# Last stage of a hybrid decoder step: the tokens divided 384/160 in the place of 272/272

## The chip, the core and the metric

The kernel runs on one core of a Trainium2 chip. The core has five engines that run side by side, each with its own stream of instructions: TensorE (PE, the matmuls, with PEld for its weight loads), VectorE (DVE), ScalarE (ACT), GpSimd (POOL) and SyncE (SP, which in this kernel issues most of the DMAs). Data lies in SBUF, matmul results in PSUM, inputs and outputs in the memory outside. The metric is the device time of one execution in microseconds (us), and less is better.

## What is computed

One layer of a decoder trunk for 512 prompt tokens and 32 sample tokens (8 sequences of 4), 544 tokens in all, with a model width of 2048 and a hidden width of 8192. What matters here is the end, the product with `w_down` and the final norm:

```
h = rms_norm(x, norm_ffn_w)
x = x + square(relu(h @ w_up)) @ w_down
y = rms_norm(x, final_norm_w)      # x * rsqrt(mean(x*x) + EPS) * w, for each token over 2048 values
```

Values are float32. The kernel gets that from products of rounded parts: a weight tile and an activation tile are each split into a high part (rounded) and a low part (the rest), and a product is three matmuls, high x high, high x low and low x high.

## The kernel before

Features lie on the 128 partitions, tokens on the free dimension. The 544 tokens are two halves of HT = 272 columns (256 prompt and 16 sample tokens each). The 2048 output features are KT = 16 blocks of 128; two blocks share a tile, `x2p[pair]`, with the layout pair member, half, token. The largest part of the product with `w_down` runs ahead of the last stage with fewer, combined products. The last stage adds what is left: four blocks of 128 hidden features (two stored activation tiles, STORED), which give `u`, four pairs of a high and a low part.

The last stage is the loop over `steps` (L1338 and on): for each half h, for each pair q of output blocks, for each of the two blocks ob:

- 12 matmuls (`product`, four hidden blocks times three parts) of 272 columns each into one bank of PSUM (`ps_small`, `ps_sm` in the trace), each matmul with its own weight load of 128 columns;
- `add` (L919): DVE adds the bank to `x2[ob][:, h]`, after which the bank is free;
- ACT squares the sum (`sq`, L1349) and multiplies it by the norm's weight (L1350);
- POOL adds the squares up in `ssq` (L1354), except those of the last two blocks, which stay separate.

The pool `small` has four banks, given out in turn, to the norms too. So output k can start when the addition of output k - 4 is done, one step earlier behind a norm.

`rstd_rows` is the norm of a half: three full-precision matmuls with a matrix of ones sum the squares over the partitions (each matmul is two records in the trace), ACT does Ln and Exp (L179, L180), DVE one refining step in four instructions (L181 to L184). Then `finish` (L1317 and on) multiplies a pair of blocks by the result, 2 x 272 columns on DVE (L1319), and SP stores it (L1320): eight multiplies and eight stores for each half. The norm of half 0 is written behind the second output of half 1, and its multiplies and stores between the later outputs. The norm of half 1, its eight multiplies and its eight stores come behind the last product.

The weights (`last_weight`, tile `w_raw`, split by ACT L992 and DVE L993) are loaded and split during half 0 and kept for half 1. A scheduler sets the order in which each engine gets its instructions, from its own estimates; `urgent()` gives what it holds a higher priority. An engine takes its instructions in that order.

Of the kernel before, what the change touches and what calls it, by code (L numbers as in the profile page):

```python
# [13 lines left out]
AF = mybir.ActivationFunctionType  # L14
ALU = mybir.AluOpType
MUL, ADD, SUB, MIN, MAX = ALU.mult, ALU.add, ALU.subtract, ALU.min, ALU.max
PSUM, DRAM = bass.MemoryType.PSUM, bass.MemoryType.DRAM

P = 128
D = 2048  # L20
KT = D // P
# [3 lines left out]
HT = HP + HS  # L25
# [3 lines left out]
EPS = 1e-6  # L29
# [12 lines left out]
STORED = [2, NF - 1]  # L42
SPAN, RING = 6, 8
RAMP = [0, 0, 2, 2, 4, 4, 6, 6]
W_OUT_ORDER = [0, 1, 2, 3, 4, 5, 8, 9, 10, 11, 12, 13, 6, 7, 14, 15]


def ahead(items, load, depth=2):

    items, queue = list(items), []  # L50
    for i, it in enumerate(items):
        while len(queue) < min(depth + 1, len(items) - i):
            queue.append(load(items[i + len(queue)]))
        yield it, queue.pop(0)
# [3 lines left out]
def trunk(ctx, tc, a):  # L58
    nc = tc.nc
# [35 lines left out]
    def tile_in(p, name, shape, dt=F32, tag=None, bufs=None):  # L95
        return p.tile(shape, dt, tag=tag or name, name=name, bufs=bufs)
# [3 lines left out]
    def ln_exp(force=False):  # L100
        if force or table[0] != "ln_exp":
            tc.keep_in_program_order(S.preload_act_table_set("natural_log_exp_and_others"))
            table[0] = "ln_exp"
# [27 lines left out]
    def ps_small(n=512):  # L131
        return tile_in(small, "ps_sm", [P, 512], tag="sm")[:, :n]
# [38 lines left out]
    def rstd_rows(out, ssqs, t, halves=(0, 1)):  # L171

        for h in halves:
            pr = ps_small(HT)
            for i, q in enumerate(ssqs):
                PE.matmul(pr, ones, q[:, h, :], start=i == 0, stop=i == len(ssqs) - 1)
            y, th = out[:, h, :], t[:, h, :]
            ln_exp()
            S.activation(y, pr, AF.Ln, bias=eps_t, scale=1.0 / D)  # L179
            S.activation(y, y, AF.Exp, scale=-0.5)  # L180
            V.tensor_tensor(th, y, y, MUL)  # L181
            V.scalar_tensor_tensor(th, pr, EPS * D, th, ADD, MUL)
            V.tensor_scalar(th, th, -0.5 / D, 1.5, MUL, ADD)
            V.tensor_tensor(y, y, th, MUL)  # L184

    def rsqrt_cols(y, x, t):

# [1113 lines left out]
             lambda key: [combos(key[1][1] + k) for k in range(key[1][2])], down_out)  # L1301


    u = []
    for m in STORED:
        x = [tile_in(cmb2, "ux", [P, 2, HT], tag="c") for _ in range(2)]
        for i in range(2):
            nc.sync.dma_start(x[i], u_d[m][:, 2 * i : 2 * i + 2])
        for i in range(2):
            hi, lo = c_tile(hlp, "ul"), c_tile(hlp, "ul")  # L1310
            parts_into(hi, lo, x[i])
            u.append(tuple((t[:, 1], t[:, 0]) for t in (hi, lo)))
    r3 = r1
    ssq = tile_in(cmb2, "ssq3", [P, 2, HT], tag="c")
    sqs = [[ssq], [ssq]]

    def finish(h, pair):  # L1317
        t = x2p[pair][:, :, h, :]
        V.tensor_tensor(t, t, r3[:, h : h + 1, :].broadcast_to([P, 2, HT]), MUL)  # L1319
        nc.sync.dma_start(a["o_y"][pair][:, :, h, :], t)  # L1320

    w_2 = []

    def last_weight(q):

        if len(w_2) < KT:
            with urgent():
                raw = tile_in(rawp, "w_raw", [P, 1024])
                nc.sync.dma_start(raw, a["w_d2"][q])
                for j in range(2):  # L1330
                    src = raw[:, 512 * j : 512 * j + 512]
                    hi, lo = (c_tile(hlp if len(w_2) < 12 else cmb, n).rearrange("p a b -> p (a b)")[:, :512]
                              for n in ("w2_hi", "w2_lo"))
                    parts_into(hi, lo, src)
                    w_2.append((hi, lo))
        return w_2[2 * q : 2 * q + 2]

    steps = [(h, q) for h in range(2) for q in range(KT // 2)]  # L1338
    for (h, q), ws in ahead(steps, lambda it: last_weight(it[1]), 1):
        for j in range(2):  # L1340
            ob = 2 * q + j
            x = x2[ob][:, h]
            ps = ps_small(HT)
            for k in range(4):
                product({h: ps}, ws[j], k * P, u[k], k == 0, k == 3, (h,))
            add(x, ps)
            sq = tile_in(cmb2, "sq", [P, 2, HT], tag="c")
            with urgent():
                S.activation(sq[:, h], x, AF.Square)  # L1349
                S.activation(x, x, AF.Copy, scale=nv[:, 32 + ob : 33 + ob])  # L1350
            if ob == 0:
                G.tensor_copy(ssq[:, h, :], sq[:, h])
            elif ob < KT - 2:
                G.tensor_tensor(ssq[:, h, :], ssq[:, h, :], sq[:, h], ADD)  # L1354
            else:
                sqs[h].append(sq)
            if h == 1 and ob == 1:
                rstd_rows(r3, sqs[0], tile_in(cmb2, "rt", [P, 2, HT], tag="c"), (0,))
            elif h == 1 and ob % 2:
                finish(0, ob // 2 - 1)  # L1360
    finish(0, KT // 2 - 1)
    with urgent():
        rstd_rows(r3, sqs[1], tile_in(cmb2, "rt", [P, 2, HT], tag="c"), (1,))
    for o in range(KT // 2):
        finish(1, o)

# [130 lines left out]
```

## Time and profile before

| | us |
|---|---|
| median of 3 runs | 2433.86 (2429.49 to 2435.54) |
| the profiled execution | 2434.44 |
| its span | 2432.7 |
| TensorE busy in the span | 2385.1 (98%) |
| VectorE busy | 1809.2 (74%) |
| ScalarE busy | 1078.2 (44%) |
| GpSimd busy | 494.7 (20%) |
| last product issued | about 2417.6 after the start of the span |
| first multiply of the last norm | 2422.49 |

A profile shows one execution. "Busy" counts a matmul from its start to a modelled end, and matmuls overlap, so what a matmul costs in a row of matmuls is the distance between two starts. Where an engine was idle before an instruction, the row names in brackets what ended the wait. Times of rows are us from the start of the span.

### The profile page before, as it was taken

The numbers are of one execution on the slowest core, as the hardware profiler recorded it, in microseconds if no ns is written. First come the engines' busy times: TensorE is split into PE (matmuls) and PEld (weight loads), VectorE is DVE, ScalarE is ACT, GpSimd is POOL, SyncE is SP. The second block draws the span as 40 slices with busy tenths as digits, with TensorE's granted clock in tenths as the row PEclk, the third lists the DMA queues.
The fourth block names the chain that finished last, engine by engine and source line by source line (L and its number), as shares of the span: only waits on it lengthen the run. The fifth ranks groups of instructions, "written<-read, shape, count | busy, mean of one in ns | idle before, by whom it ended". The sixth has DMA issues, their size and how long they took to land.

```text
span 2432.7 us, 47364 instructions
## 1 busy us (share of the span) xinstructions
PE 2385.1 (98%) x19089; PEld 2358.4 (97%) x19089; DVE 1809.2 (74%) x2937; ACT 1078.2 (44%) x1598; POOL 494.7 (20%) x776
## 2 busy tenths in 40 slices
PE   9999999999999999998999999999999999999997
PEld 8999999999999999998999999999999999999997
DVE  9676676666657635888888888888578888888885
ACT  6424332432432424555555555555323333333445
POOL 5123213312412204310010111101401212121003
PEclk9999999999999999999999999999999999999999
DMA  6243333333333546565555555556945656565433
GB/s 203 93 115 117 98 112 109 118 98 96 126 94 108 179 127 206 189 214 192 193 193 201 201 199 187 182 191 214 391 133 169 229 165 227 160 218 152 139 94 111
DMA packets 144275, 397.96 MB, mean 164 GB/s; under 512 B 35348, under 2 KB 44216, under 8 KB 144056
## 3 DMA queue, kind: packets, MB, share of 16 engines
q1 hardware_dynamic: 108648, 266.12, 34.9%
q0 software_dynamic: 35408, 128.82, 14.1%
q8 instruction: 150, 2.46, 0.4%
q14 instruction: 69, 0.57, 0.1%
HBM read 317.37 MB, written 77.49 MB: 162 GB/s over the span
## 4 chain that ended last, share of the span: by engine, by line
PE 86%; DVE 5%; DMA 5%; ACT 2%; issue 1%; SPq 0%; DVEq 0%; POOLq 0%; ACTq 0%; POOL 0%
PE ps_s L76 49%; PE ps_big L76 30%; PE ps_sm L76 7%; DVE w_lo L145 2%; DMA w_raw<-in_w_o_dram 2%; DMA w_raw<-in_w_up_dram 2%; ACT w_hi L142 1%; DMA w_q<-in_w_up_dram 1%; DMA w_raw<-in_w_d_dram 1%; DVE x L1004 1%; DMA xr<-in_x_dram 0%; PE ps_sm L80 0%; DVE x_lo L160 0%; DVE w_lo L1130 0%; ACT w_hi L1129 0%
## 5 line engine op out<-in xcount | busy, mean ns | idle before, releaser
L1129 ACT ACTIVATE w_hi<-w_q 128x768 fp32r<-128x768 f32 (+3 forms) x422 | 375.1, 889 | 559.0 <-PE ps_s L76 466.1
L76 PE MATMUL ps_s<-uc,w_hi 128*128 128x272 f32 x3136 | 593.1, 289 | 6.9 <-ACT w_hi L1129 6.3
L76 PEld LDWEIGHTS ps_s<-uc,w_hi 128*128 128x128 f32 x3136 | 491.1, 188 | 10.6 <-ACT w_hi L1129 8.9
L1130 DVE TENSOR_TENSOR w_lo<-w_q,w_hi 128x768 fp32r<-128x768 f32 (+3 forms) x422 | 425.3, 1008 | 65.0 <-ACT w_hi L1129 63.5
L76 PE MATMUL ps_s<-uc,w_lo 128*128 128x272 f32 x1568 | 450.2, 288 | 0.0
L76 PE MATMUL ps_big<-x_hi,w_hi 128*128 128x272 f32 x2016 | 425.9, 292 | 0.6 <-ACT x_hi L157 0.5
L76 PE MATMUL ps_big<-x_hi,w_lo 128*128 128x272 f32 x2016 | 418.3, 289 | 2.6 <-DVE w_lo L145 2.6
L76 PE MATMUL ps_big<-x_lo,w_hi 128*128 128x272 f32 x2016 | 419.0, 289 | 0.3 <-DVE x_lo L160 0.3
L142 ACT ACTIVATE w_hi<-w_raw 128x1024 fp32r<-128x1024 f32 (+3 forms) x215 | 211.4, 983 | 432.4 <-PE ps_big L76 287.0
L145 DVE TENSOR_TENSOR w_lo<-w_raw,w_hi 128x1024 fp32r<-128x1024 f32 (+3 forms) x215 | 277.6, 1291 | 148.1 <-ACT w_hi L142 143.6
L76 PEld LDWEIGHTS ps_big<-x_hi,w_hi 128*128 128x128 f32 x2016 | 316.6, 188 | 5.1 <-ACT x_hi L157 1.7
L76 PEld LDWEIGHTS ps_big<-x_hi,w_lo 128*128 128x128 f32 x2016 | 315.5, 188 | 3.5 <-DVE w_lo L145 3.4
L76 PEld LDWEIGHTS ps_big<-x_lo,w_hi 128*128 128x128 f32 x2016 | 317.0, 189 | 0.7 <-DVE x_lo L160 0.5
L76 PEld LDWEIGHTS ps_s<-uc,w_lo 128*128 128x128 f32 x1568 | 294.9, 188 | 0.3 <-DVE w_lo L1130 0.3
L76 PE MATMUL ps_s<-c_hi,w_hi 128*128 128x272 f32 x928 | 267.3, 288 | 5.9 <-ACT w_hi L1129 5.7
L76 PE MATMUL ps_s<-c_hi,w_lo 128*128 128x272 f32 x928 | 268.2, 289 | 1.4 <-DVE w_lo L145 0.7
L76 PE MATMUL ps_s<-c_lo,w_hi 128*128 128x272 f32 x928 | 267.1, 288 | 0.0
L919 DVE TENSOR_TENSOR x2v<-x2v,ps_s 128x272 f32<-128x272 f32 x326 | 140.1, 434 | 74.1 <-PE ps_s L76 72.3
L1229 POOL DMA_DIRECT2D uc<-ucd x196 | 106.2, 547 | 432.7 <-PE ps_s L76 414.7
L76 PEld LDWEIGHTS ps_s<-c_hi,w_hi 128*128 128x128 f32 x928 | 175.5, 189 | 6.4 <-ACT w_hi L1129 5.9
L76 PEld LDWEIGHTS ps_s<-c_hi,w_lo 128*128 128x128 f32 x928 | 175.1, 189 | 2.1 <-DVE w_lo L1130 1.2
L76 PEld LDWEIGHTS ps_s<-c_lo,w_hi 128*128 128x128 f32 x928 | 175.1, 189 | 0.0
(375 smaller groups left out, 4223.2 us busy)
## 6 DMA issues: line engine op xcount, KB each, us to landing
w_q<-in_w_up_dram SPq DMA_DIRECT2D x116, 512.0 KB, 5.0
w_raw<-in_w_in_dram SPq DMA_DIRECT2D x106, 512.0 KB, 3.4
uc<-ucd POOLq DMA_DIRECT2D x196, 272.0 KB, 5.9
w_q<-in_w_d_dram SPq DMA_DIRECT2D x128, 384.0 KB, 3.3
w_raw<-in_w_o_dram SPq DMA_DIRECT2D x32, 512.0 KB, 3.7
ucd<-u_hi POOLq DMA_DIRECT2D x28, 544.0 KB, 5.7
ucd<-tc POOLq DMA_DIRECT2D x28, 544.0 KB, 6.8
w_raw<-in_w_up_dram SPq DMA_DIRECT2D x28, 512.0 KB, 3.6
```

The costliest lines, as they stand in the source:

```text
L76: return cls.held(nc.tensor.matmul(*args, **kw))
L142: S.activation(hi[:, c], raw[:, c], AF.Copy)
L145: V.tensor_tensor(lo[:, c], raw[:, c], hi[:, c].bitcast(F32), SUB)
L919: V.tensor_tensor(out, out, ps, ADD)
L1004: V.scalar_tensor_tensor(x2[o][:, h], x2[o][:, h], nv[:, KT + o : KT + o + 1], r2[:, h], MUL, MUL)
L1129: S.activation(hi, s, AF.Copy)
L1130: V.tensor_tensor(lo, s, hi.bitcast(F32), SUB)
L1229: nc.gpsimd.dma_start(t.bitcast(F32), uc_d[KS[j]][:, 2 * b : 2 * b + 2])
```

## The change

The last stage no longer divides the tokens at 272. Its first part has the columns 0 to 383 of the 544, its second part the 160 that remain. To take a slice of any width, the pair of halves is read as one row of 544 columns (`flat`). Products, additions, squares, sums, norms, multiplies and stores of the stage go by these parts: the same number of instructions, with 384 columns where the first half had 272 and 160 where the second half had 272. `rstd_rows` is cut in two, with the body for one slice in `rstd`. The stored activations were kept with the halves exchanged. They are now put in order as they are loaded, so that four loads of 2 x 272 columns become eight of 272.

```
+CUT = 384
...
+    def rstd(y, ssqs, th, n):
+        pr = ps_small(n)
+        for i, q in enumerate(ssqs):
+            PE.matmul(pr, ones, q, start=i == 0, stop=i == len(ssqs) - 1)
+        ln_exp()
...
         for i in range(2):
-            nc.sync.dma_start(x[i], u_d[m][:, 2 * i : 2 * i + 2])
+            for h in range(2):
+                nc.sync.dma_start(x[i][:, h], u_d[m][:, 2 * i + 1 - h])
         for i in range(2):
             hi, lo = c_tile(hlp, "ul"), c_tile(hlp, "ul")
             parts_into(hi, lo, x[i])
-            u.append(tuple((t[:, 1], t[:, 0]) for t in (hi, lo)))
-    r3 = r1
-    ssq = tile_in(cmb2, "ssq3", [P, 2, HT], tag="c")
+            u.append((flat(hi), flat(lo)))
+    r3 = flat(r1)
+    ssq = flat(tile_in(cmb2, "ssq3", [P, 2, HT], tag="c"))
     sqs = [[ssq], [ssq]]
-
-    def finish(h, pair):
-        t = x2p[pair][:, :, h, :]
-        V.tensor_tensor(t, t, r3[:, h : h + 1, :].broadcast_to([P, 2, HT]), MUL)
-        nc.sync.dma_start(a["o_y"][pair][:, :, h, :], t)
+    PARTS = (slice(0, CUT), slice(CUT, 2 * HT))
+
+    def finish(v, pair):
+        c = PARTS[v]
+        t = x2p[pair].rearrange("p j h t -> p j (h t)")[:, :, c]
+        V.tensor_tensor(t, t, r3[:, c].unsqueeze(1).broadcast_to([P, 2, c.stop - c.start]), MUL)
+        nc.sync.dma_start(a["o_y"][pair].rearrange("p j h t -> p j (h t)")[:, :, c], t)
...
-            ps = ps_small(HT)
-            for k in range(4):
-                product({h: ps}, ws[j], k * P, u[k], k == 0, k == 3, (h,))
+            ps = ps_small(c.stop - c.start)
+            whi, wlo = ws[j]
+            for k, (xhi, xlo) in enumerate(u):
+                for i, (wp, xp) in enumerate(((whi, xhi), (whi, xlo), (wlo, xhi))):
+                    PE.matmul(ps, wp[:, k * P : (k + 1) * P], xp[:, c], start=k == i == 0, stop=k == 3 and i == 2)
             add(x, ps)
...
-            if h == 1 and ob == 1:
-                rstd_rows(r3, sqs[0], tile_in(cmb2, "rt", [P, 2, HT], tag="c"), (0,))
-            elif h == 1 and ob % 2:
+            if v == 1 and ob == 1:
+                last_norm(0)
+            elif v == 1 and ob % 2:
                 finish(0, ob // 2 - 1)
     finish(0, KT // 2 - 1)
     with urgent():
-        rstd_rows(r3, sqs[1], tile_in(cmb2, "rt", [P, 2, HT], tag="c"), (1,))
+        last_norm(1)
```

The scheduler gives some instructions another order. On DVE, behind the norm of the first part, this stood before (L919 is the addition of an output of the second part, with `ps_sm` as its bank; L1319 is the final multiply of a pair of the first part):

```order
L182 SCALAR_TENSOR_TENSOR rt_28317<-ps_sm_28318,rt_28317 128x272
L919 TENSOR_TENSOR x2v1_19950<-x2v1_19950,ps_sm_28328 128x272
L183 TENSOR_SCALAR rt_28317<-rt_28317 128x272
L184 TENSOR_TENSOR r1_91<-r1_91,rt_28317 128x272
L1319 TENSOR_TENSOR x2v0_19948<-x2v0_19948,r1_91 128x2x272
L919 TENSOR_TENSOR x2v1_19950<-x2v1_19950,ps_sm_28346 128x272
L1319 TENSOR_TENSOR x2v1_19950<-x2v1_19950,r1_91 128x2x272
L919 TENSOR_TENSOR x2v2_19952<-x2v2_19952,ps_sm_28366 128x272
L1319 TENSOR_TENSOR x2v2_19952<-x2v2_19952,r1_91 128x2x272
L1319 TENSOR_TENSOR x2v3_19954<-x2v3_19954,r1_91 128x2x272
L919 TENSOR_TENSOR x2v2_19952<-x2v2_19952,ps_sm_28384 128x272
```

Additions and multiplies alternate: after the norm, one or two multiplies stand between two additions. At the same place on DVE there is now this (L922 the addition, L1326 the multiply):

```order
L187 TENSOR_TENSOR r1_91<-r1_91,rt_28321 128x384
L1326 TENSOR_TENSOR x2v0_19948<-x2v0_19948,r1_91 128x2x384
L922 TENSOR_TENSOR x2v1_19950<-x2v1_19950,ps_sm_28332 128x160
L1326 TENSOR_TENSOR x2v1_19950<-x2v1_19950,r1_91 128x2x384
L1326 TENSOR_TENSOR x2v2_19952<-x2v2_19952,r1_91 128x2x384
L1326 TENSOR_TENSOR x2v3_19954<-x2v3_19954,r1_91 128x2x384
L922 TENSOR_TENSOR x2v1_19950<-x2v1_19950,ps_sm_28350 128x160
L1326 TENSOR_TENSOR x2v4_20171<-x2v4_20171,r1_91 128x2x384
L1326 TENSOR_TENSOR x2v5_20173<-x2v5_20173,r1_91 128x2x384
L1326 TENSOR_TENSOR x2v6_20175<-x2v6_20175,r1_91 128x2x384
L1326 TENSOR_TENSOR x2v7_20177<-x2v7_20177,r1_91 128x2x384
L922 TENSOR_TENSOR x2v2_19952<-x2v2_19952,ps_sm_28370 128x160
```

The eight multiplies have only two additions among them, and the addition that stood among the norm's refining steps now stands behind the first multiply.

On TensorE, in the products of the very last output, the sums of squares of the second norm (`ones`) stood so before (`ul` with `w2` is a product, `ssq3` the sum of POOL, `sq` the square of output 14):

```order
L76 MATMUL ps_sm_28573<-ul_27894,w2_hi_28207 128x272
L76 MATMUL ps_sm_28595<-ssq3_27914,ones_87 128x272
L76 MATMUL ps_sm_28573<-ul_27895,w2_hi_28207 128x272
L76 MATMUL ps_sm_28573<-ul_27894,w2_lo_28208 128x272
L76 MATMUL ps_sm_28573<-ul_27898,w2_hi_28207 128x272
L76 MATMUL ps_sm_28573<-ul_27899,w2_hi_28207 128x272
L76 MATMUL ps_sm_28595<-sq_28570,ones_87 128x272
```

Four products lie between the two sums. There they stand so now:

```order
L77 MATMUL ps_sm_28577<-ul_27896,w2_hi_28211 128x160
L77 MATMUL ps_sm_28599<-ssq3_27918,ones_87 128x160
L77 MATMUL ps_sm_28577<-ul_27897,w2_hi_28211 128x160
L77 MATMUL ps_sm_28599<-sq_28574,ones_87 128x160
L77 MATMUL ps_sm_28577<-ul_27896,w2_lo_28212 128x160
```

One product lies between them. The rest of the products follows as before.

## Rows read from the trace of the kernel before

**Rows 1.** The page: the span of the profiled execution.
```profile
span 2432.7 us, 47364 instructions
```

**Rows 2.** Stages: stretch, us, busy us (instructions) of each engine, clock, DMA, GB/s.
```profile
2364.50:2390.60 26.10, 26.10 (x209) 26.10 (x209) 19.23 (x37) 20.51 (x46) 11.26 (x14) 1.00 0.42 141
2390.60:2417.90 27.30, 26.91 (x205) 26.07 (x203) 15.37 (x29) 16.09 (x35) 11.22 (x14) 1.00 0.24 83
...
2422.50:2432.70 10.20, 0.00 (x0) 0.00 (x0) 5.16 (x8) 0.00 (x0) 0.00 (x0) 0.50 0.63 219
```

**Rows 3.** Timeline of TensorE at four places: start us, us, what, count.
```profile
62.88 1.28 PE L76 MATMUL ps_sm<-sel,abr 64*128 64x16 f32 x10
...
62.88 0.50 PE L76 MATMUL ps_sm<-sel,abr 64*128 64x16 f32 x3
...
109.25 0.28 PE L76 MATMUL ps_sm<-kq_hi 128*128 128x256 f32 x1
...
109.96 0.41 PE L76 MATMUL ps_big<-x_hi,w_hi 128*128 128x272 f32 x2
...
236.31 0.39 PE L76 MATMUL ps_sm<-nl,ones_r 128*128 128x512 f32 x1
...
236.77 0.39 PE L76 MATMUL ps_sm<-nl,ones_r 128*128 128x512 f32 x1
...
2371.04 0.29 PE L76 MATMUL ps_sm<-ul,w_lo 128*128 128x272 f32 x1
...
2374.05 0.29 PE L76 MATMUL ps_sm<-ul,w_lo 128*128 128x272 f32 x1
```

**Rows 4.** Weight loads by shape: count, busy us, mean ns of one, idle before.
```profile
L76 PEld LDWEIGHTS ps_sm<-ul,w_hi 128*128 128x128 f32 x256 | 40.3, 188 | 0.2
...
L76 PEld LDWEIGHTS ps_sm<-s,km 128*64 128x64 f32 x128 | 13.8, 137 | 1.2
```

**Rows 5.** Timeline of TensorE at the two norms.
```profile
2393.75 0.62 PE L76 MATMUL ps_sm<-ssq,ones 128*128 128x272 f32 x2
...
2395.37 0.29 PE L76 MATMUL ps_sm<-ul,w_lo 128*128 128x272 f32 x1
...
2415.29 0.73 PE L76 MATMUL ps_sm<-ssq,ones 128*128 128x272 f32 x2 [0.35 <-POOL ssq L1354]
```

**Rows 6.** Timeline of DVE and POOL at the final multiplies.
```profile
2398.39 1.30 DVE L1319 TENSOR_TENSOR x2v<-x2v,r 128x544 f32<-128x544 f32 x1
...
2398.33 0.77 POOL L1354 TENSOR_TENSOR ssq<-ssq,sq 128x272 f32<-128x272 f32 x1 [2.50 <-ACT sq L1349]
...
2422.49 5.17 DVE L1319 TENSOR_TENSOR x2v<-x2v,r 128x544 f32<-128x544 f32 x8
```

**Rows 7.** The chain that ended last, behind the last product: start us, us, what.
```profile
2417.89 0.45 DVE x2v L919
...
2418.43 0.44 ACT sq L1349
...
2418.91 0.74 PE ps_sm L76 x2
...
2419.67 0.50 ACT r L179
...
2422.49 0.73 DVE x2v L1319
```

**Rows 8.** Instructions on `ul`: ns min/median/max, first and last start, form.
```profile
L992 ACT ACTIVATE ul<-ux x4: 641/642/644, 2301.9 to 2309.0; 128x544 fp32r<-128x544 f32 x4
L993 DVE TENSOR_TENSOR ul<-ux,ul x4: 718/718/718, 2302.9 to 2311.9; 128x544 fp32r<-128x544 f32 x4
```

**Rows 9.** SP's last stores, and stretches in which their data starts and ends (DMA share).
```profile
2423.28 5.33 SPq L1320 DMA_DIRECT2D out_o_y_dram<-x2v  x8
...
2424.00:2425.00 1.00, 0.00 (x0) 0.00 (x0) 1.00 (x2) 0.00 (x0) 0.00 (x0) 0.50 0.52 181
...
2430.00:2431.00 1.00, 0.00 (x0) 0.00 (x0) 0.00 (x0) 0.00 (x0) 0.00 (x0) 0.50 0.71 235
```

More of the change, by code (lines that the diff above doesn't have):

```diff
@@ L173, in rstd_rows @@
         for h in halves:
[L174 to L184, printed above, removed]
+            rstd(out[:, h, :], [q[:, h, :] for q in ssqs], t[:, h, :], HT)
+    def rstd(y, ssqs, th, n):
[3 more added lines that the diff above has]
+        ln_exp()
+        S.activation(y, pr, AF.Ln, bias=eps_t, scale=1.0 / D)
+        S.activation(y, y, AF.Exp, scale=-0.5)
+        V.tensor_tensor(th, y, y, MUL)
+        V.scalar_tensor_tensor(th, pr, EPS * D, th, ADD, MUL)
+        V.tensor_scalar(th, th, -0.5 / D, 1.5, MUL, ADD)
+        V.tensor_tensor(y, y, th, MUL)
     def rsqrt_cols(y, x, t):
@@ L1301, in trunk @@
              lambda key: [combos(key[1][1] + k) for k in range(key[1][2])], down_out)
+    flat = lambda t: t.rearrange("p h t -> p (h t)")
     u = []
@@ L1311, in trunk, with last_norm @@
             parts_into(hi, lo, x[i])
-            u.append(tuple((t[:, 1], t[:, 0]) for t in (hi, lo)))
-    r3 = r1
-    ssq = tile_in(cmb2, "ssq3", [P, 2, HT], tag="c")
+            u.append((flat(hi), flat(lo)))
+    r3 = flat(r1)
+    ssq = flat(tile_in(cmb2, "ssq3", [P, 2, HT], tag="c"))
     sqs = [[ssq], [ssq]]
-    def finish(h, pair):
-        t = x2p[pair][:, :, h, :]
-        V.tensor_tensor(t, t, r3[:, h : h + 1, :].broadcast_to([P, 2, HT]), MUL)
-        nc.sync.dma_start(a["o_y"][pair][:, :, h, :], t)
+    PARTS = (slice(0, CUT), slice(CUT, 2 * HT))
[4 more added lines that the diff above has]
+        nc.sync.dma_start(a["o_y"][pair].rearrange("p j h t -> p j (h t)")[:, :, c], t)
+    def last_norm(v):
+        c = PARTS[v]
+        t = flat(tile_in(cmb2, "rt", [P, 2, HT], tag="c"))[:, c]
+        rstd(r3[:, c], [q[:, c] for q in sqs[v]], t, c.stop - c.start)
     w_2 = []
@@ L1336, in last_weight @@
         return w_2[2 * q : 2 * q + 2]
-    steps = [(h, q) for h in range(2) for q in range(KT // 2)]
-    for (h, q), ws in ahead(steps, lambda it: last_weight(it[1]), 1):
+    steps = [(v, q) for v in range(2) for q in range(KT // 2)]
+    for (v, q), ws in ahead(steps, lambda it: last_weight(it[1]), 1):
+        c = PARTS[v]
         for j in range(2):
             ob = 2 * q + j
-            x = x2[ob][:, h]
-            ps = ps_small(HT)
-            for k in range(4):
-                product({h: ps}, ws[j], k * P, u[k], k == 0, k == 3, (h,))
+            x = flat(x2[ob])[:, c]
+            ps = ps_small(c.stop - c.start)
[3 more added lines that the diff above has]
+                    PE.matmul(ps, wp[:, k * P : (k + 1) * P], xp[:, c], start=k == i == 0, stop=k == 3 and i == 2)
             add(x, ps)
-            sq = tile_in(cmb2, "sq", [P, 2, HT], tag="c")
+            sq = flat(tile_in(cmb2, "sq", [P, 2, HT], tag="c"))
             with urgent():
-                S.activation(sq[:, h], x, AF.Square)
+                S.activation(sq[:, c], x, AF.Square)
                 S.activation(x, x, AF.Copy, scale=nv[:, 32 + ob : 33 + ob])
             if ob == 0:
-                G.tensor_copy(ssq[:, h, :], sq[:, h])
+                G.tensor_copy(ssq[:, c], sq[:, c])
             elif ob < KT - 2:
-                G.tensor_tensor(ssq[:, h, :], ssq[:, h, :], sq[:, h], ADD)
+                G.tensor_tensor(ssq[:, c], ssq[:, c], sq[:, c], ADD)
             else:
-                sqs[h].append(sq)
-            if h == 1 and ob == 1:
-                rstd_rows(r3, sqs[0], tile_in(cmb2, "rt", [P, 2, HT], tag="c"), (0,))
-            elif h == 1 and ob % 2:
+                sqs[v].append(sq)
+            if v == 1 and ob == 1:
+                last_norm(0)
+            elif v == 1 and ob % 2:
                 finish(0, ob // 2 - 1)
```

## The prediction

> **What bounds the kernel now.** I read the span first [rows 1], then the last stage in three stretches [rows 2]: products of half 0 (in the first 26.1 us), of half 1 (27.3 us, TensorE busy 26.91), and the end, 10.2 us in which TensorE does nothing and DVE is busy for half. TensorE is granted its full 2.4 GHz in the first two (1.00). So up to 2417.9 the price of a product counts, and behind it a chain of single instructions and a queue of stores. Product prices stand in the TensorE timeline [rows 3]: a matmul starts where the one before it lets go, so the distance of two starts is the price, not the duration shown. 24 products of 272 columns lie between 2371.04 and 2374.05: 125.4 ns each. Six of 256 columns take 0.71 us, 118 ns each. Two of 512 columns take 0.46 us, 229 ns each. Between these a column costs about 0.43 ns. The small ones are another matter: ten matmuls with 16 columns take 1.28 us, the first three of them 0.50, so seven steps take 0.78 us, 112 ns each, with next to nothing to stream. What they share with the products is a weight tile of 128 columns. Its load lasts 188 ns, one of 64 columns 137 ns [rows 4]: 0.8 ns a column, about 102 ns for 128, and a fixed part that overlaps. So I read 112 ns as the floor of a step whose weights are 128 columns wide. It has never shown in this kernel's products because 256 columns or more are longer.
>
> **The change, part by part.** All times are of the profiled execution (2434.44 us, span 2432.7), which lies 0.6 us above the median of the runs, 2433.86.
>
> *Products of the first part.* 192 matmuls go from 272 to 384 columns. On the line from 125.4 to 229 ns, 384 lies at 125.4 + 112/240 x 103.6 = 173.7 ns. 192 x 48.3 ns = **+9.3 us**. From below, at 0.4167 ns a column (one column a cycle at the granted 2.4 GHz), it is +9.0. All of it is on the path, since TensorE is the bound here. ACT and DVE split weights beside it, with more time for each output than before.
>
> *Products of the second part.* 192 matmuls go from 272 to 160 columns. If they follow their columns the line gives 118 - 96 x 0.434 = 76 ns; with the floor it is 112 ns; from above, no cheaper than now, 125.4, unless narrow matmuls run in more passes (a rival below). I take 112, since those steps have the same weight width, and the products load new weights for each matmul: 192 x 13.4 ns = **-2.6 us**, with -9.5 and 0 as ends. This is the core of the forecast: the columns taken out of part 2 hardly come back as time, those put into part 1 are paid in full.
>
> The Trainium skill has a rule that speaks against this: "TensorE: Matmul & The Clock Gate", section "Back-to-back issue gap", puts an isolated gap at N/2.4 + 2.5 ns, in which the weight load has no share. An estimate by it: 384 + 160 cost the same as 272 + 272 (162.5 + 69.2 against 2 x 115.8 ns), and this and the last paragraph together come to zero. The rows say 125.4 where that rule has 115.8.
>
> *Norms.* A norm has three full-precision matmuls, six records. In the middle of half 1 they and two products take from 2393.75 to 2395.37, 1.62 us, so 0.457 us for each of the three [rows 5], in proportion to columns. Norm 0 grows by 3 x 0.19, the two of norm 1 that lie in the product stream shrink by 2 x 0.19: **+0.2 us**. Their order shifts too: the square of output 14 is now wanted behind one product instead of four. TensorE waited 0.35 us for POOL's sum there [rows 5]; it will now wait some 0.45 for the square. **+0.1**.
>
> *A wait in part 2.* The order of DVE shows it. After the first norm, the eight final multiplies of part 1 stand almost in one piece: one, the addition of output 2, three, the addition of output 3, four, the addition of output 4. Every addition frees one of four PSUM banks, and output k needs the bank of output k - 4. A multiply of 544 elements takes 0.65 us when nothing is beside it (5.17 for eight, [rows 6]), one of 768 then 0.91. From the start of part 2: two outputs 2.7 us (12 x 112 ns each), norm matmuls 1.94 to 4.65, Ln and Exp (0.59 and 0.53 with 0.09 for 112 more columns, hops) to 6.0, four DVE steps of 0.42 to 0.56 to 8.2, multiply to 9.1, addition 2 to 9.45, three multiplies and addition 3 to 12.5, four and addition 4 to 16.5. TensorE meanwhile ends output 6 at 11.4. Output 7 waits 1.1 us for the bank of output 3. It ends at 13.9, and output 8 waits 2.6 for that of output 4. Before, multiplies and additions alternate, and TensorE does not stop. In addition POOL's sums stretch multiplies that run beside them: one took 1.30 us beside a POOL addition of 0.77 [rows 6]. Two narrower ones fall into this clump, some 0.4 us each. Together **+4.5 us**; the ends are 2 (additions a little earlier than I place them) and 6.
>
> *The chain behind the last product.* 112 columns are worth 0.12 us on DVE and 0.09 on ACT: 272 elements take 0.45 and 0.44, 544 take 0.72 and 0.64 [rows 7, 8]. Addition 0.12, square 0.09, last norm matmul 0.19, Ln and Exp 0.18, four DVE steps 0.46, first multiply 0.23 (0.73 before): **-1.3 us**.
>
> *Stores.* Before, eight stores are issued in 5.33 us, 0.67 each. They move 8 x 278 KB in about 6.2 us (2424.5 to 2430.7), some 360 GB/s, so transfers end 2.7 us after the last is issued [rows 9]. After, a store holds 164 KB instead of 278, about 0.5 us of transfer, less than SP needs for an issue, and DVE's 0.4 per multiply is less too. So SP paces the end: no queue stands behind the last store, which ends after 1.2 us (2423.28 to about 2424.5 in these rows) + 0.5. That is 1.7 instead of 2.7: **-1.0 us**. If issuing a narrower store were quicker it would be up to 2 us.
>
> *Loads.* Four loads of the stored activations become eight of half the size on SP, about 90 us ahead of their use. Prefetch covers it; uncovered, each extra issue would cost a few tenths. Reshaping and the norm helper cost nothing: they change addresses only.
>
> Sum: 9.3 - 2.6 + 0.2 + 0.1 + 4.5 - 1.3 - 1.0 = **+9.2 us**, so 2443.6 us for such an execution, and less 0.6, **2443.0 us**, 0.38% over the median.
>
> **The rivals.**
>
> *A. Narrow matmuls cost only their columns, the bank waits stay.* The price is 76 ns. Part 2 would begin its clump 0.9 us earlier and run its last eight outputs 3.5 us quicker, of which 1.5 goes to waiting for POOL's sum of squares before the last norm. About 3 us less than forecast: 2440.0. For it speaks that no product in this trace is narrow; against it, the steps of 112 ns.
>
> *B. The other side: no floor and no bank wait.* The mechanism is a weight load that hides under a matmul of any width, with DVE's additions coming in time. Products are 9.3 - 9.5, and chain and stores give 2.3: with norms and one us of wait for POOL about -1.3, 2432.5 us, not slower. It decides from a narrow product of 88 ns or less: 7.2 us over 192 matmuls is then saved, which pays for the rest. By the Trainium skill's gap rule, named above, the estimate would be 2429. Against it speak the floor and DVE's order, both of which must be wrong.
>
> *C. Narrow matmuls of this type need more passes.* The norm's full-precision matmul costs 0.457 us for 272 columns, 1.68 ns a column, four times the products' rate. Were the products below 256 columns run like that, 160 columns would cost 0.27 us: 192 x 0.144 = +27.8 instead of -2.6, and no bank waits, since an output then takes 3.2 us. 9.3 + 27.8 + 0.2 - 2.3 = +35 us, 2468.3. For it: every product in the trace has 256 columns or more, so none shows otherwise. Against: the width is no part of the type, and loads look alike in both (188 ns).
>
> *D. The change does not do what it says*: a norm, or the stores, wait for something that I do not see, and the time stays near 2434.
>
> **How the numbers follow.** Forecast 0.70, A 0.10, B 0.04, C 0.13, D 0.03. What a measurement of this kernel tells from no change is about 0.3%, 7.3 us: below 2426.6 is faster, above 2441.2 slower. The forecast itself may lie between 2438 (wait of 2, chain and stores at their best) and 2449 (no gain in part 2, wait of 6, noise of the runs); some 0.57 of its 0.70 are above 2441.2. With 0.03 of A and all of C, slower is 0.73. Faster is 0.03, of B and noise. Same is 0.24. The range holds forecast and A with the spread of the runs, 2437 to 2451; C is left out, with B and D.
>
> **What would show it.** In the profile after: starts of products of 384 columns 174 ns apart, and of 160 columns 112 ns apart (76 for A, about 270 for C); two gaps of TensorE, of 1 and 2.5 us, behind outputs 6 and 7 of part 2, ended by DVE's addition, with multiplies in a block beside them; about 3.5 us in place of 4.6 from last product to first multiply; stores still 0.67 us apart, and the data's end 1.7 us after the last issue. The forecast is wrong if narrow products are priced otherwise, or if additions come early enough to leave the banks free.

## The result and the profile after

| | us |
|---|---|
| 272/272, median | 2432.68 (2429.49 to 2435.69) |
| 384/160, median | 2450.25 (2448.32 to 2458.11) |
| ratio | 1.0078, 95% interval 1.0060 to 1.0096 |
| the profiled execution of 384/160 | 2454.99 |

It is slower, as forecast, but by 17.6 us where 9.2 were forecast. From the first product of the last stage to the end of the span 68.4 us have become 87.4: all of it, and 1.4 us more, lies in this stage (the stage itself begins 1.6 us later in this execution).

The stages of the changed kernel, as [rows 2] had them of before (stretch, us, busy us and instructions of each engine, granted clock, DMA share, GB/s). The second row is part 2 up to its first stop, the third what lies behind the second stop, the fourth the end.

```profile
2365.80:2402.00 36.20, 36.20 (x212) 35.95 (x211) 21.80 (x38) 24.80 (x47) 14.19 (x14) 1.00 0.31 103
2402.00:2413.30 11.30, 11.30 (x91) 10.49 (x90) 6.29 (x11) 4.44 (x10) 1.52 (x3) 1.00 0.07 26
...
2418.70:2440.30 21.60, 21.60 (x100) 21.45 (x100) 2.88 (x10) 8.08 (x22) 5.22 (x10) 0.50 0.12 43
2444.70:2453.20 8.50, 0.00 (x0) 0.00 (x0) 3.29 (x8) 0.00 (x0) 0.00 (x0) 0.50 0.51 154
```

The third row is the surprise: the last 96 products of part 2, and the four records of two sums of the norm, at a granted clock of 0.50, with TensorE busy all the time. In the kernel before that clock showed in this stage only behind the last matmul [rows 2].

TensorE's timeline, first products of 384 columns (answering [rows 3]), then the two stops of part 2 and what follows them:

```profile
2379.70 0.34 PE L77 MATMUL ps_sm<-ul,w_lo 128*128 128x384 f32 x1
...
2382.86 0.34 PE L77 MATMUL ps_sm<-ul,w_lo 128*128 128x384 f32 x1
```

```profile
2412.28 0.39 PE L77 MATMUL ps_sm<-ul,w_hi 128*128 128x160 f32 x2
...
2413.17 0.28 PE L77 MATMUL ps_sm<-ul,w_lo 128*128 128x160 f32 x1
2414.65 0.45 PE L77 MATMUL ps_sm<-ul,w_hi 128*128 128x160 f32 x2 [1.20 <-DVE x2v L922]
...
2415.95 0.41 PE L77 MATMUL ps_sm<-ul,w_lo 128*128 128x160 f32 x1
2418.70 0.71 PE L77 MATMUL ps_sm<-ul,w_hi 128*128 128x160 f32 x2 [2.33 <-DVE x2v L922]
2419.21 0.41 PE L77 MATMUL ps_sm<-ul,w_lo 128*128 128x160 f32 x1
...
2420.49 0.41 PE L77 MATMUL ps_sm<-ul,w_lo 128*128 128x160 f32 x1
```

18 steps of 384 columns take 3.16 us, 176 ns each. Eight steps of 160 columns ahead of the first stop take 0.89 us, 111 ns each. Then TensorE starts nothing from 2413.17 to 2414.65 and from 2415.95 to 2418.70: less one step of 0.11 each, two stops of 1.37 and 2.64 us. Behind the second, six steps take 1.28 us, 213 ns each.

The same stretch in the chain that ended last shows who holds TensorE: DVE's multiplies in a block, with the additions (L922) that free the banks between them.

```profile
2410.24 0.96 DVE x2v L1326
2411.20 0.23 DVE x2v L922
2411.43 2.94 DVE x2v L1326 x3
2414.37 0.23 DVE x2v L922
2414.60 3.81 DVE x2v L1326 x4
2418.41 0.24 DVE x2v L922
...
2418.70 22.02 PE ps_sm L77 x100
...
2440.73 0.33 DVE x2v L922
...
2441.54 0.92 PE ps_sm L77 x2
...
2444.69 0.49 DVE x2v L1326
```

And the granted clock (last column but two) between the stops and from the second one on:

```profile
2414.65:2415.94 1.29, 1.29 (x11) 1.29 (x12) 1.29 (x2) 0.77 (x2) 0.68 (x1) 1.00 0.93 335
2415.94:2418.70 2.76, 0.43 (x4) 0.21 (x3) 2.76 (x5) 0.00 (x0) 0.00 (x0) 0.50 1.03 370
```

It is 1.00 between the stops and 0.50 from 2415.94 on, where the last product ahead of the second stop starts: in this execution the fall came behind the first stop, before the second had begun. A second profile of the same kernel (below) has it at 1.00 until 2417.4 and at 0.50 from 2417.5, within the second stop. So the stops were priced as lost time only; the products behind them, at twice the price, were not.

The end, answering [rows 9]: the last eight stores on SP's timeline, the last of them alone, and the stretches in which their data ends.

```profile
2445.24 5.22 SPq L1327 DMA_DIRECT2D out_o_y_dram<-x2v  x8
...
2449.90 0.56 SPq L1327 DMA_DIRECT2D out_o_y_dram<-x2v  x1
```

```profile
2451.00:2451.80 0.80, 0.00 (x0) 0.00 (x0) 0.00 (x0) 0.00 (x0) 0.00 (x0) 0.50 0.69 218
2451.80:2453.00 1.20, 0.00 (x0) 0.00 (x0) 0.00 (x0) 0.00 (x0) 0.00 (x0) 0.50 0.00 0
```

The issues still begin 0.67 us apart, so SP paces them. The last begins at 2449.90 and the data has ended by 2451.8, 1.9 us later, where the prediction, which counted from the same point, said 1.7. In the kernel before, the last begins at 2427.95 and the data ends by 2430.9, 2.9 us later.

### The profile page after: what moved, and what is told of

The parts are those of the page before. It is cut to its first block, busy times and chain, and to the rows that moved or that the text cites. A ratio compares the mean times of both kernels' runs of the same rounds, so it can differ in the third digit from the quotient of the medians.

```text
span 2453.2 us, 47383 instructions
## 1 busy us (share of the span) xinstructions
PE 2407.1 (98%) x19089; PEld 2377.3 (97%) x19089; DVE 1806.6 (74%) x2937; ACT 1079.0 (44%) x1598; POOL 494.9 (20%) x776
## 4 chain that ended last, share of the span: by engine, by line
PE 85%; DMA 6%; DVE 6%; ACT 2%; issue 1%; SPq 0%; ACTq 0%; DVEq 0%; POOL 0%
PE ps_s L77 48%; PE ps_big L77 30%; PE ps_sm L77 7%; DVE w_lo L146 2%; DMA w_raw<-in_w_o_dram 2%; DMA w_raw<-in_w_up_dram 2%; ACT w_hi L143 1%; DMA w_q<-in_w_d_dram 1%; DMA w_q<-in_w_up_dram 1%; DVE w_lo L1133 0%; DVE x2v L1326 0%; ACT w_hi L1132 0%; PE ps_sm L81 0%; DVE x L1007 0%; DMA w_raw<-in_w_d_dram 0%
## 5 line engine op out<-in xcount | busy, mean ns | idle before, releaser
L1133 DVE TENSOR_TENSOR w_lo<-w_q,w_hi 128x768 fp32r<-128x768 f32 (+3 forms) x422 | 424.5, 1008 | 60.5 <-ACT w_hi L1132 58.9
L922 DVE TENSOR_TENSOR x2v<-x2v,ps_s 128x272 f32<-128x272 f32 x326 | 139.7, 433 | 74.9 <-PE ps_s L77 73.4
```

Of the source, the lines that this page charges most:

```text
L922: V.tensor_tensor(out, out, ps, ADD)
L1133: V.tensor_tensor(lo, s, hi.bitcast(F32), SUB)
```

## The experiments

The theory after the result: **(1)** the stops of TensorE let the granted clock fall, and the narrow products behind them do not bring it back. The rival: **(2)** narrow products lose the clock by themselves (or with DVE's block of multiplies beside them), stop or not. The whole time of an execution moves by some 4 us either way through what lies ahead of the last stage, so beside the ratio the table has two lengths from the profiled execution: from the first to the last start of a product on `ul` in the last stage, and from the first of them to the end of the span. Two values are two profiles of the same kernel. The ratio is to runs of the 272/272 kernel taken along with each kernel, whose medians lie between 2428.84 and 2432.99 us.

| kernel | median us | ratio (95%) | first to last product | first product to end | clock from the stop to the last product |
|---|---|---|---|---|---|
| 272/272 | | | 53.3, 53.4 | 68.4, 68.5 | no stop, 1.00 |
| 384/160 | 2450.25 | 1.0078 (1.0060 to 1.0096) | 74.4, 74.4 | 87.4, 87.4 | 0.50 |
| more banks | 2440.57 | 1.0036 (1.0021 to 1.0051) | 65.5 | 78.5 | 0.50, from a late stop |
| additions in order | 2435.03 | 1.0005 (0.9995 to 1.0015) | 60.5 | 73.0 | no stop, 1.00 |
| 272/272 with blocks of four | 2434.37 | 1.0005 (0.9995 to 1.0014) | 54.8 | 69.9 | 1.00 |
| 288/256 | 2432.68 | 0.9998 (0.9989 to 1.0008) | 53.2 | 67.6 | no stop, 1.00 |
| 272/272, block of eight | 2435.87 | 1.0013 (1.0003 to 1.0023) | 55.3 | 70.4 | 1.00 |
| 384/160, one stop | 2439.59 | 1.0038 (1.0016 to 1.0059) | 72.9, 71.5 | 85.8, 84.5 | 0.50 in the profiles |
| 384/160, stops filled | 2446.42 | 1.0053 (1.0033 to 1.0073) | 64.6, 64.6 | 77.1, 77.1 | no stop, 1.00 |
| 272/272, longer stop | 2444.16 | 1.0059 (1.0036 to 1.0083) | 59.6 | 74.7 | 0.50 for 3.4 us, then 1.00 |

### More banks

```
-            ps = ps_small(c.stop - c.start)
+            ps = (tile_in(small2, "ps_b", [P, 512], tag="sm2")[:, : c.stop - c.start] if v and ob % 2
+                  else ps_small(c.stop - c.start))
```

> The 384/160 kernel, with the odd outputs of the second part in the four banks of another pool, so that output k waits for the addition of output k - 8 instead of k - 4. DVE keeps its block of multiplies. Theory 1 (the two stops of TensorE, 1.4 and 2.6 us, let the granted clock fall, and the half clock behind them costs some 10 us): no stop before the norm, clock 1.00 up to the last product, narrow products 112 ns apart to the end, 2450 - 4 - 10 = 2436 us, and at most 2439. Theory 2 (narrow products bring the clock down by themselves, stop or not): the clock falls to 0.50 somewhere in part 2 without a stop, products there 213 ns apart, 2445 us or more.

Stretches of part 2: before a stop, the stop, and behind it; then the row of TensorE's timeline at its end.

```profile
2396.50:2417.70 21.20, 21.20 (x180) 20.34 (x178) 13.98 (x27) 9.46 (x25) 5.37 (x10) 1.00 0.42 150
2417.70:2420.80 3.10, 0.40 (x4) 0.31 (x3) 0.00 (x1) 2.40 (x8) 2.09 (x4) 1.00 0.00 0
2420.90:2425.90 5.00, 4.80 (x23) 4.58 (x22) 0.32 (x1) 0.76 (x2) 0.00 (x0) 0.50 0.00 0
```

```profile
2420.49 0.56 PE L77 MATMUL ps_sm<-ssq,ones 128*128 128x160 f32 x2 [2.70 <-POOL ssq L1370]
```

The time came within 2 us of the upper figure of theory 1, but not in the way expected. The bank waits are gone, and narrow products ran for 21.2 us beside the whole block of multiplies at 1.00: that is against theory 2. But the additions that the block holds up hold up ACT's squares and POOL's sums too. Output 14 is finished early, the norm's first sum then waits 2.70 us for POOL, and with this stop, among narrow products, the clock falls for the two dozen products that are left.

### Additions in order

The multiplies of part 1 and the additions of part 2 are held on DVE in their written order, so that they alternate:

```
-        V.tensor_tensor(t, t, r3[:, c].unsqueeze(1).broadcast_to([P, 2, c.stop - c.start]), MUL)
+        m = V.tensor_tensor(t, t, r3[:, c].unsqueeze(1).broadcast_to([P, 2, c.stop - c.start]), MUL)
+        if not v:
+            tc.keep_in_program_order(m)
...
-            add(x, ps)
+            if v:
+                tc.keep_in_program_order(V.tensor_tensor(x, x, ps, ADD))
+            else:
+                add(x, ps)
```

> The 384/160 kernel, with the additions of the second part and the final multiplies of the first held on DVE in the order in which they are written: behind the norm an addition, an addition, a multiply, and so on, never two multiplies in a row. The four banks stay. Theory 1 (the stops bring the clock down): stops below half a us, clock 1.00 up to the last product, 2436 to 2439 us as with more banks. Theory 2 (narrow products alone): half clock in part 2, 2445 us or more. If the order costs more than the block did (a multiply of 768 elements waits for POOL), a stop of about 1 us stays, and it shows whether a shorter stop is enough for the clock to fall.

Part 2 up to the last product:

```profile
2396.40:2420.90 24.50, 24.29 (x204) 23.25 (x202) 12.36 (x26) 13.31 (x34) 8.80 (x14) 1.00 0.26 97
```

No stop and a clock of 1.00 through 24.5 us of products of 160 columns. The stage takes 73.0 us, 14.4 less than in the changed kernel with the same widths. The order of DVE alone is worth that.

### 272/272 with blocks of four, and with a block of eight

Here the widths stay as before, and DVE's order makes the stops (the additions of half 1 and the multiplies of half 0 held in order):

```
-            elif h == 1 and ob % 2:
-                finish(0, ob // 2 - 1)
-    finish(0, KT // 2 - 1)
+            elif h == 1 and ob in (2, 3):
+                for o in range(4 * (ob - 2), 4 * (ob - 1)):
+                    finish(0, o)
```

> The 272/272 kernel, with the eight final multiplies of the first half held on DVE in blocks of four, so that the additions of outputs 3 and 4 come late and TensorE stops for banks in the midst of products of 272 columns. Theory 1a (any stop of one or two us lets the clock fall, and it stays down for as long as in the 384/160 kernel): products 213 to 250 ns apart behind the stop, + 3 for the stops and + 10 or more for the clock, 2446 us or more. Theory 1b (the clock falls only where the products around the stop are narrow, or comes back soon with wide ones): + 1 to 5 us, 2434 to 2438 us, clock 1.00 or low for a few us only.

The stop and the rest of the products:

```profile
2408.20:2409.40 1.20, 0.01 (x1) 0.00 (x0) 1.20 (x4) 0.00 (x0) 0.00 (x0) 1.00 1.01 348
2409.40:2423.00 13.60, 13.25 (x100) 12.88 (x100) 4.05 (x10) 9.53 (x22) 7.70 (x10) 1.00 0.12 42
```

TensorE stopped once, for about 1.2 us, and the clock stayed at 1.00 in this execution; the ten timed runs have a mean clock of 0.995 to 0.997, like those of the kernel before. The second kernel does all eight multiplies behind addition 2 (`elif h == 1 and ob == 2`, then `for o in range(KT // 2)`, which is eight):

> The 272/272 kernel with the eight final multiplies of the first half held in one block on DVE, so that TensorE, in products of 272 columns, stops once for about 4 us (1.2 us with blocks of four, where the clock stayed at 1.00). Theory 1a (a stop that is long enough lets the clock fall whatever the width, and the products' width decides whether it comes back): a fall at or behind the stop; if it comes back within 7 us: + 4 to 7 us, 2437 to 2440 us; if it stays down for the some 80 products left (250 ns each instead of 125): + 4 + 10, 2447 us. Theory 1b (only narrow products let the clock fall): 1.00 throughout, + 4 us, 2437 us.

The stop was 1.77 us and not 4: the multiplies run from 2400.24 to 2405.9, but up to 2404.5 TensorE still had products for which a bank was free. These are what follows the stop, and TensorE's timeline at its end:

```profile
2406.40:2421.50 15.10, 14.75 (x112) 14.38 (x112) 4.47 (x11) 10.49 (x24) 8.49 (x11) 1.00 0.16 55
```

```profile
2406.39 0.52 PE L76 MATMUL ps_sm<-ul,w_hi 128*128 128x272 f32 x2 [1.77 <-DVE x2v L1349]
```

The clock was 1.00 again, and the stage is longer by the stop alone: 70.4 us against 68.5. So in these two profiles a stop of this size, among products of 272 columns, cost no clock. In the timed runs of both kernels the mean clock (0.995 to 0.997) leaves no room for a fall that lasts to the last product; a fall of a few us would not show in it.

### 288/256

> The 384/160 kernel with the tokens divided 288/256, so that no product is narrower than 256 columns and all else of the change (loads, layout, norm by slices) stays. By the products' prices of the 272/272 kernel: 192 x (132.3 - 125.4) = + 1.3 us in the first part, 192 x (118 - 125.4) = - 1.4 us in the second, chain and stores - 0.3: the time of the 272/272 kernel within 2 us, clock 1.00 up to the last product. If it is 5 us or more slower, the cost of the change lies in something else than the widths (the loads, the order).

The diff is one number (`CUT = 288`). The stage takes 67.6 us, 0.8 less than before, of which 0.7 lies behind the last product; the ratio cannot be told from 1. All else that the change brought (loads, layout, norm by slices) costs nothing that can be measured: only the widths and the order that follows from them do. This is also the fastest version that I have, and it does not beat the kernel before by anything that a measurement can tell.

### The changed kernel again

> The 384/160 kernel once more, for a second profile. Theory 1 (the stops bring the clock down): the same two stops of about 1.4 and 2.7 us, the clock falling during or just behind them, and the rest of the narrow products some 213 ns apart. Rival (the fall of the clock in the first profile was a chance event, such as the falls of 3.4 or 6.8 us in other stages): clock 1.00 up to the last product, about 2440 us.

The whole run took 2454.80 us. Two stretches, up to the second stop's middle and from there to the last product, and TensorE's timeline at its end:

```profile
2413.00:2417.40 4.40, 1.80 (x15) 1.49 (x13) 4.40 (x7) 0.77 (x2) 0.69 (x1) 1.00 0.98 358
2417.50:2440.10 22.60, 21.62 (x100) 21.48 (x100) 3.86 (x12) 8.08 (x22) 5.24 (x10) 0.50 0.16 57
```

```profile
2418.48 0.71 PE L77 MATMUL ps_sm<-ul,w_hi 128*128 128x160 f32 x2 [2.47 <-DVE x2v L922]
```

The same stops, the clock falling some 1.5 us later, within the second of them, and the same 96 products at half clock. The six timed executions and this one have a mean clock of 0.990 to 0.992, where the kernel before has 0.995 to 0.997. So the changed kernel lost the clock in every execution.

### One stop

The order held as above, but with the changed kernel's first block: a multiply, addition 2, three multiplies, additions 3 and 4, then one multiply for two additions.

```
...
             if v == 1 and ob == 1:
                 last_norm(0)
-            elif v == 1 and ob % 2:
-                finish(0, ob // 2 - 1)
-    finish(0, KT // 2 - 1)
+                finish(0, 0)
+            elif v == 1 and ob == 2:
+                for o in range(1, 4):
+                    finish(0, o)
+            elif v == 1 and ob in (4, 6, 8, 10):
+                finish(0, ob // 2 + 2)
```

> The 384/160 kernel with the additions held so that only its first stop is left: behind the norm a multiply, addition 2, three multiplies, additions 3 and 4, and from there on one multiply for two additions. TensorE, in products of 160 columns, stops once for about 1.4 us before output 7. If the first stop alone was what let the clock fall (it fell 2.8 us behind its start, as the second began): half clock from there to the end, some 110 products at 213 ns, + 11 + 1.4 on the 2435 us without stops: 2446 us or more. If it takes the second stop too: 1.00 to the last product, 2436 to 2437 us.

The stop, the two us behind it, and the rest of part 2:

```profile
2406.10:2407.50 1.40, 0.20 (x3) 0.04 (x2) 1.40 (x4) 0.00 (x0) 0.00 (x0) 1.00 1.01 362
2407.50:2409.50 2.00, 2.00 (x10) 2.00 (x11) 2.00 (x5) 1.89 (x6) 1.43 (x2) 0.53 0.97 349
2409.50:2431.60 22.10, 22.10 (x104) 21.95 (x103) 4.66 (x11) 6.96 (x19) 5.89 (x10) 0.50 0.21 76
```

In this execution a single stop (TensorE waits 1.20 us in the timeline, 1.48 from start to start) cost the clock, and it did not come back in 24 us. But the timed runs fall in two groups: 2435.3, 2437.8, 2438.4 and 2439.6 us with a mean clock of 0.996 or 0.997 over the execution, and 2446.3, 2447.0 and 2452.2 with 0.990 or 0.991. So, as far as the mean clock tells, the same stop does it in some executions and not in others.

> The 384/160 kernel with the one stop of 1.5 us in its narrow products, for a second profile (its runs fell in two groups: some 2438 us with a mean clock of 0.997 and some 2447 with 0.991). Either the clock falls behind the stop as in the first profile and stays at 0.50 to the end, or it stays at 1.00 past the same stop; then the stage is some 11 us shorter (76 instead of 87.5 us), and a stop of this size is on the edge. What would speak against theory 1: half clock without a stop, or a run of the second group with clock 1.00.

It was of the second group again (2452.18 us, 0.992): 1.00 in the stop, 0.50 soon behind it, 84.5 us for the stage. A profile of the first group I do not have; that its clock stayed up is read from its mean clock, which is that of the kernel without stops.

### Stops filled with work

TensorE runs 12 and 24 products into a bank that nobody reads where it waited; DVE's block stays:

```
...
+            if v and ob in (7, 8):
+                junk = tile_in(small2, "ps_f", [P, 512], tag="sm2")[:, : c.stop - c.start]
+                for i in range(12 if ob == 7 else 24):
+                    tc.keep_in_program_order(PE.matmul(junk, whi[:, :P], u[0][0][:, c], start=True, stop=True))
...
+                    if v and ob in (6, 7, 8):
+                        tc.keep_in_program_order(mm)
```

> The 384/160 kernel, in which TensorE, while it waits for the banks of outputs 7 and 8 of the second part, runs 12 and 24 further products of 160 columns into a bank that nobody reads (about 1.3 and 2.7 us at 112 ns). DVE's order and the arrival of the additions stay. Theory 1 (standing still is what lets the clock fall): 1.00 up to the last product, the added products take the place of the stops, and the time is the first result less the half clock: 2450 - 10 = 2440 us. Theory 2 (narrow products, or DVE's block of multiplies beside them, bring the clock down): half clock as before, 2450 us or more.

The stretch of the former stops and the rest of part 2, then the fillers in TensorE's timeline:

```profile
2406.50:2412.00 5.50, 5.50 (x51) 5.48 (x50) 5.50 (x9) 0.82 (x3) 0.68 (x1) 1.00 1.00 358
2412.00:2423.70 11.70, 11.59 (x101) 11.25 (x100) 2.80 (x10) 7.83 (x22) 5.29 (x10) 1.00 0.21 78
```

```profile
2406.50 1.50 PE L77 MATMUL ps_f<-ul,w_hi 128*128 128x160 f32 x12
...
2409.27 2.85 PE L77 MATMUL ps_f<-ul,w_hi 128*128 128x160 f32 x24
```

The same 96 products, with the four records of the norm, take 11.7 us here and 21.6 in the changed kernel. This is the run that decides: widths, DVE's block, stores and the arrival of the additions are those of the changed kernel (on DVE, additions 2, 3 and 4 start 3.18 and 4.04 us apart in both), TensorE loses the same time, and only its standing still is gone. The stage is 10.3 us shorter.

Its runs as a whole do not agree as well: this profiled one took 2437.93 us, three more 2446.1 to 2446.9, all with a mean clock of 0.996 or 0.997.

> The 384/160 kernel with products in the place of its stops, for a second profile: its first run took 2437.9 us and three others some 2446.5 us, all at a mean clock of 0.996 or 0.997. If theory 1 holds, the last stage takes 77 us again from its first product to the end with the clock at 1.00 up to the last product, whatever the whole run takes, and a longer run has its additional time ahead of that stage. If the additional 8.5 us lie in the last stage, stops filled with work cost something that I have not seen.

The second profile (2439.53 us) has the stage at 77.1 us again, with a clock of 1.00. None of the long runs left a profile. Where their 8.5 us are stays open; their mean clock speaks against half clock. So the gain of 10.3 us is shown for the stage; by the medians of whole runs the filling gave back 3.8 us.

### A longer stop in wide products

The block of eight with four more multiplies behind it, into a tile that nobody reads; products of 272 columns.

```
...
+                junk = tile_in(cmb2, "rt", [P, 2, HT], tag="c")
+                for o in range(4):
+                    tc.keep_in_program_order(V.tensor_tensor(junk, x2p[0][:, :, 0, :], x2p[1][:, :, 0, :], MUL))
```

> The 272/272 kernel with the block of eight multiplies, and four more multiplies into a tile that nobody reads behind them, so that TensorE stops once for about 4.5 us (1.8 to 2.05 us without them, where the clock stayed at 1.00 in all runs) in products of 272 columns. If the length of the stop is all that counts, the clock falls here as in the 384/160 kernel; if it then stays at 0.50 through the some 110 products left, + 4.5 + 13 on the 2433 us: 2450 us; if products of 272 columns bring it back in 3.4 to 7 us, + 4.5 + 2 to 3.5: 2440 us. If only narrow products lose the clock: 1.00 throughout, 2438 us.

The stop, the stretch of half clock and the rest, then TensorE's timeline behind the stop:

```profile
2403.50:2407.60 4.10, 0.04 (x1) 0.00 (x0) 4.00 (x7) 0.00 (x0) 0.00 (x0) 1.00 1.05 359
2407.70:2411.10 3.40, 2.87 (x12) 2.87 (x13) 1.52 (x5) 2.83 (x8) 2.10 (x3) 0.50 0.01 4
2411.20:2424.60 13.40, 13.05 (x101) 12.68 (x99) 3.50 (x8) 7.80 (x17) 6.29 (x9) 1.00 0.00 1
```

```profile
2408.23 0.82 PE L76 MATMUL ps_sm<-ul,w_hi 128*128 128x272 f32 x2 [4.69 <-DVE x2v L1349]
...
2409.08 0.66 PE L76 MATMUL ps_sm<-ul,w_hi 128*128 128x272 f32 x2
...
2410.44 0.66 PE L76 MATMUL ps_sm<-ul,w_hi 128*128 128x272 f32 x2
```

A stop of 4.69 us costs the clock here too. But a dozen products of 272 columns later (six steps take 1.36 us, 227 ns each) it is back at 1.00, and the fall is worth some 1.2 us (12 products at 0.10 us more): the stage is 6.2 us longer, of which the stop is 4.7. In the changed kernel 96 products of 160 columns, with TensorE busy all the time, did not bring it back. So the 10 us have two conditions: a stop that lowers the clock, and products behind it that leave it low.

Among products of 272 columns the clock falls behind shorter stops too, but not in every execution. In an earlier stage, some 1740 us from the start, TensorE waits 1.88 to 2.52 us for weights among products of 272 columns. In eight of the fourteen profiles the clock fell within 1.7 us behind this stop, for 3.41 us each time, and in six it did not fall. Behind a stop of 1.48 or 1.49 us, some 15 us later in the same stage, it fell in none of the fourteen. The changed kernel shows both for the first of these: in its first profile the stop is 2.23 us and ends at 1742.48, in its second it is 2.21 us and ends at 1742.23. The stretch of half clock in the first, and the same place in the second:

```profile
1743.51:1746.92 3.41, 3.41 (x17) 3.41 (x16) 2.03 (x6) 1.64 (x3) 1.82 (x4) 0.50 1.03 385
```

```profile
1742.20:1750.00 7.80, 7.68 (x53) 7.00 (x54) 5.67 (x13) 3.10 (x7) 4.45 (x10) 1.00 1.04 386
```

### The kernel before again

> The 272/272 kernel once more, for a second profile: the time from the first product of the last stage to the end of the span should be 68.5 us again, while the start of the stage may lie some us elsewhere. If the stage itself varies by more than 1 us, the differences of stages between kernels that I read are no better than that.

2435.11 us, and 68.5 us for the stage against 68.4. The stage repeats within some 0.1 us; whole runs do not.

## Why the prediction was wrong in size

The sum of the prediction without stops of TensorE is 9.3 - 2.6 + 0.2 + 0.1 - 1.3 - 1.0 = +4.7 us. The kernel with the additions in order is just that case: its stage is 73.0 - 68.5 = +4.5 us. Term by term:

- *Products and norms up to the last product:* +7.0 forecast, 60.5 - 53.4 = +7.1 measured. A product of 384 columns took 176 ns (174 forecast), one of 160 columns 111 at full clock (112). The floor that was read from matmuls of 16 columns [rows 3] holds for 160, and it refutes rivals A (76 ns), B (88 or less) and C (270). The Trainium skill, "TensorE: Matmul & The Clock Gate", section "LDWEIGHTS (loading the stationary operand)", puts a load at its columns over 1.2 in ns. An estimate by it is 107 ns for 128 columns, and the step of 111 ns measured here lies 4 ns above it. That section is what the prediction should have set against the gap rule that it cited, which leaves the weight load out.
- *The waits for banks:* +4.5 forecast, 1.1 and 2.6 us for the two stops and 0.8 for multiplies that POOL's sums stretch; the stops measure 1.37 and 2.64, with 0.95 to 0.98 us for a multiply in the block (0.91 forecast). With the stops filled the stage is 77.1 - 73.0 = 4.1 us over the one without.
- *Chain and stores:* -2.3 forecast. From the last product's start to the end of the span 15.1 us were, and 12.5 are, with the additions in order: -2.6. From the last addition to the first multiply it is 3.6 us at a full clock (3.5 forecast, 4.6 before, [rows 7]), and 3.96 in the changed kernel, where the last norm matmul runs at half clock (0.92 us against 0.74 with 272 columns).
- *The clock, which has no term:* the prediction took 112 ns for all 192 products of part 2 (its second step, -2.6), after reading 1.00 as the clock of both halves [rows 2]. That held for the 96 ahead of the second stop. The 96 behind it took 213 ns: 96 x 0.10 = 9.8 us. The stage with its stops filled differs from the changed one by 87.4 - 77.1 = 10.3 us, these and the last norm.

So the failed step is the price of the second part's products behind the stops, or, said from the other side, the price of a stop: it was taken as its length (4 us), where it was its length and half the clock behind it (14 us). 4.5 + 4.1 + 10.3 = 18.9 us is what the stage shows; the medians of whole runs differ by 17.6.

Could the profile of before have told? In part. It has no stop of TensorE that is longer than half a us among the products of this stage, and no product below 256 columns. But its last stretch shows the clock at 0.50 [rows 2], where TensorE had stood still for a while. And in an earlier stage it shows a fall in the midst of products, which the prediction did not look for: two waits for weights of 1.62 and 0.74 us, then half clock for 3.41 us, then full clock again.

```profile
1044.22 0.40 PE L76 MATMUL ps_sm<-c_hi,w_hi 128*128 128x272 f32 x1 [1.62 <-ACT w_hi L142]
...
1045.48 0.39 PE L76 MATMUL ps_sm<-c_hi,w_lo 128*128 128x272 f32 x1 [0.74 <-DVE w_lo L145]
```

```profile
1046.37:1049.78 3.41, 3.41 (x18) 3.41 (x17) 3.41 (x6) 3.38 (x7) 0.00 (x0) 0.50 0.46 154
1049.78:1055.00 5.22, 5.22 (x44) 5.22 (x44) 5.20 (x10) 3.17 (x6) 2.13 (x4) 1.00 0.94 291
```

So that stops can bring the clock down could be read there; that products of 160 columns do not bring it back could not. A forecast that adds stops of 1 and 2.6 us to a stream has to ask whether that can happen in the midst of it, and the two answers (1.00 or 0.50 behind the stop) should have been ends of the range: 2443 and some 2453.

The Trainium skill has a case near this one: the same page, section "A second HAM failure mode: psum-queue depth-cycling", tells of a kernel in which short idle times of TensorE between groups, as it goes round its PSUM banks, bring the clock down and up again. The trace agrees on the fall behind bank waits. It differs on what follows: products of 160 columns stayed at 0.50 to the last one in the changed kernel.

Rival D fell too: the change did what it said. Direction and chances (0.73 for slower) were right. The range reached to 2451, which is 17.1 us above the median that it started from (2433.86); the change measured 17.6, and single runs lay up to 7 us beyond the range. Two figures of the rivals were added up wrongly, without weight for the rest: C's 9.3 + 27.8 + 0.2 - 2.3 = +35 us gives 2468.9 and not 2468.3, and B's 2429 sets the new widths at the rule's price against the old width at the row's 125.4 ns; with the rule for both it is 2432.8.

## What to carry to other kernels

Where matmuls are narrower than their weight load takes, columns taken away bring nothing (112 ns at 160 columns as at 16), and uneven parts pay for the wide one in full. Before a cut makes matmuls shorter, look at the order on the engine that frees their banks: the additions that one output waits for must come as often as outputs do, and a scheduler's block of long multiplies between them is a stop. Price a stop of TensorE with the clock behind it: here 4 us of stops cost 14 in the stage, and putting the additions in order took all 14 back, giving TensorE something to do 10.

## What I had not expected of the hardware

- Half clock nearly doubles the step of 160 columns too, which does not follow its columns: 213 ns against 111, and 227 against 125 for 272 columns.
- The clock came back within a dozen products of 272 columns, and not at all in 96 of 160 columns, though TensorE was busy for 21.60 of 21.60 us. Widths in between were not run.
- The same stop costs the clock in some executions and not in others. Among narrow products that gives the kernel with one stop of 1.2 us two times, with medians of 2438 and 2447 us by the mean clock of its runs. Among products of 272 columns it is a matter of 3.41 us at half clock: stops of 2.23 and 2.52 us had it, one of 2.48 us did not, those of 1.2 and 1.77 us made above did not in the one profile of each, and that of 1.48 us in none of fourteen.
